# A two-layer hybrid decoder step: head loads in quarters, the table stage in fewer steps, chunks by way of DRAM and held norm products

## Chip, cores, metric

One core of one Trainium2 chip runs the whole step as one program. The metric is the device time of that program in microseconds (us), as the median of several runs; lower is better. Of the core's engines these matter here: TensorE (PE) for products and transposes, VectorE (DVE) and ScalarE (ACT) for elementwise work, GpSimd (POOL) for a few small operations, SyncE (SP), which issues most of the transfers.

## What is computed

The reference is one inference step of two layers on 256 prompt tokens and 8 x 8 sample tokens, in fp32. One layer, cut to what matters:

```
x  += 0.5 * SwiGLU_1(rms(x))
z   = rms(x) @ w_in            -> u (512) | q (512) | k (128) | v (128)
y_ssm  = GLU(gelu(Re(C h_t) + D u_t)),  h_t = Abar h_{t-1} + Bbar u_t   # 32 groups x 16 channels, 64 complex states each
y_attn = sliding-window attention over 128 keys, 8 heads, a sink per head
x  += concat(rms(y_ssm), rms(y_attn)) @ w_out
x  += 0.5 * SwiGLU_2(rms(x))
x  += (p @ w_ple_proj) * sigmoid(rms(x) @ w_ple_gate)
```

Then a final RMS norm. The width is 1024, the FFN's 2816. Besides the tokens' outputs the last keys and values and the last states are returned.

## The kernel before

All 320 tokens (256 + 64) lie along the free axis, channels on the 128 partitions, so x is 8 tiles of 128x320. To keep fp32 accuracy each weight block and each input is split into a high and a low part, and a 128x128 block of a product takes three PE instructions (mm3, lines 182 to 184: high x high, high x low, low x high), here called products. A weight tile of 128x1024 is loaded by SP into one of four raw buffers (wfetch, line 150), ACT makes the high part (line 163), DVE the low one (line 164), two tiles ahead of use.

A norm (class Norm, line 190) is not applied ahead of a product. ACT squares each tile (line 210), DVE adds the squares (line 216), and finish sums over partitions with three tiny PE products (line 244); DVE scales (line 247), POOL takes the power -1/2 (line 249), and three transposes spread the result over partitions (line 267). The spread is placed behind LATER = 22 further products, and the result multiplies the products' outputs when they are evacuated. For the two output norms in the mixer (attn_norm, ssm_norm, lines 929 and 934) the inputs themselves are scaled, so the following products depend on the spread.

Each layer runs FFN1, mixer, FFN2 and the per-layer embedding (ple). The FFN (line 272) has two halves of 11 blocks: gate and up products, then 8 down blocks. The S5 tables (powers of Abar, the block-Toeplitz table tt, the input table wb, the output table wc) are made by a generator, prep, in small steps, one after each FFN block (step, line 145): layer 0's beside FFN1, layer 1's beside FFN2 of layer 0. It writes tables to DRAM (wb_d, wc_d, kt_d, tt_d); tt_d is first filled with zeros, and then eight copies of ever shorter pieces go into it. At its end come doublings of cosine and sine tables (ect, est, lines 579 to 584) and a correction that renormalizes both (lines 590 to 595).

In the mixer (mix, line 601) tokens are grouped in chunks of 8: 40 chunks. u, evacuated as u2 (channel on partitions), must become U, where a partition is (position in the chunk, channel in the group). chunk_in does this on PE, per 8 groups: 8 transposes (line 669), two ACT copies, 8 transposes (line 674), an ACT copy; then the table products with wb (line 680). rotate (line 693) is a chain of ten DVE operations per 8 groups that turns these, scans over chunks and gives the states H. chunk_out multiplies U and H with tt and wc (line 872), transposes back (line 883) and applies D, gelu and a split. Attention runs in six units, four prompt and two sample: scores, softmax, flip (transposes of the probabilities), mix.

The string MIXSEQ sets the order in which all this is written: p0 to p9 are blocks of the input projection (q0: p0 and p1 together), i chunk_in, r rotate, s, f, m scores, flip and mix of a unit, y a step of chunk_out, z the ple projection, g the GLU, a and n the output norms, A and S the output projection, t and w table loads, v value transposes, x the load of p. Tile's scheduler then puts the instructions of each engine in one fixed order, which follows the written order closely but not exactly.

At the start x comes in three pieces (lines 1017 to 1026), the first weight in two halves, and POOL squares and adds the tiles of the first norm (line 1030).

## Time and profile before

| | us |
|---|---|
| median of 3 runs | 1287.34 (1287.19 to 1287.66) |
| the profiled execution | 1286.57 |
| its span in the profile | 1284.8 |
| PE busy | 1257.4 (98%) |
| DVE busy | 911.0 (71%) |
| ACT busy | 598.9 (47%) |
| POOL busy | 81.5 (6%) |

Busy time overlaps between engines. A PE instruction's shown duration (0.31 us for a product) is longer than the distance between two of them, since they are pipelined: what a product costs is read from the distance of starts, or from the number of products in a window without waits. The granted clock in a window is a share of 2.4 GHz; where it is 0.50 the clock was 1.2 GHz. The records of the clock begin at its first change, so the windows show 1.00 ahead of it whatever it was; there the distance of products tells.

### The profile page before, as it was taken

Reading aid. Unit: us, or ns where it says so; the run is one execution under the profiler, and the core shown is the slowest. Engines: PE = TensorE matmul, PEld = TensorE weight load, DVE = VectorE, ACT = ScalarE, POOL = GpSimd, SP = SyncE. Lnnn points to the kernel's source line nnn. Section 1 sums busy time; section 2 is a strip of 40 time slices with the busy share of each in tenths; the row PEclk is TensorE's granted clock in tenths of the full one; section 3 lists DMA queues with packets and bytes.
Section 4 is the critical chain, followed back from the end, with each engine's and each line's share of the span. In section 5 each row is a group of like instructions: output and inputs, shape, how many; then the busy total and the mean of one; then the engine's idle time right before and its main releaser. Section 6 shows DMA issues by size and latency. Waiting matters only on the chain.

```text
span 1284.8 us, 22994 instructions
## 1 busy us (share of the span) xinstructions
PE 1257.4 (98%) x9153; PEld 1231.1 (96%) x9153; DVE 911.0 (71%) x1609; ACT 598.9 (47%) x984; POOL 81.5 (6%) x96
## 2 busy tenths in 40 slices
PE   7999999899999999999999999999999999999996
PEld 7999999898899999999999999999888999999996
DVE  6588776978786878788785555557877755555575
ACT  5443433455764443344653333345476543333454
POOL 4300002001004000010000000000000000000000
PEclk9999999999999999999999999999999999999998
DMA  7836666354254468654444454345432444454351
GB/s 251 314 125 204 240 208 212 120 197 144 76 192 147 150 194 256 219 189 141 166 174 151 129 154 174 136 115 188 164 106 99 147 151 135 142 180 141 113 174 41
DMA packets 74620, 210.62 MB, mean 164 GB/s; under 512 B 8545, under 2 KB 18497, under 8 KB 74481
## 3 DMA queue, kind: packets, MB, share of 16 engines
q1 hardware_dynamic: 72560, 203.22, 47.8%
q0 software_dynamic: 1664, 5.28, 1.3%
q8 instruction: 72, 1.18, 0.4%
q10 hardware_dynamic: 288, 0.66, 0.1%
q14 instruction: 36, 0.29, 0.1%
HBM read 191.78 MB, written 19.69 MB: 165 GB/s over the span
## 4 chain that ended last, share of the span: by engine, by line
PE 89%; DVE 6%; issue 3%; ACT 1%; POOL 1%; DMA 0%; SPq 0%; POOLq 0%; DVEq 0%; ACTq 0%
PE pt L182 17%; PE pt L184 17%; PE pt L183 17%; PE pc L182 11%; PE pc L184 11%; PE pc L183 11%; DVE wl L164 2%; PE pa L872 1%; PE pa L500 1%; POOL r L249 1%; DVE s L704 0%; DVE s L703 0%; DMA xa<-xT 0%; PE pa L883 0%; PE pa L244 0%
## 5 line engine op out<-in xcount | busy, mean ns | idle before, releaser
L163 ACT ACTIVATE wh<-wr 128x1024 fp32r<-128x1024 f32 (+3 forms) x365 | 350.9, 963 | 556.3 <-issue 302.0
L184 PE MATMUL pt<-big,wl 128*128 128x320 f32 x1584 | 492.6, 311 | 4.3 <-DVE wl L164 4.3
L182 PE MATMUL pt<-big,wh 128*128 128x320 f32 x1584 | 493.4, 312 | 0.0
L183 PE MATMUL pt<-big,wh 128*128 128x320 f32 x1584 | 492.2, 311 | 0.0
L164 DVE TENSOR_TENSOR wl<-wr,wh 128x1024 fp32r<-128x1024 f32 (+3 forms) x365 | 403.1, 1107 | 100.5 <-ACT wh L163 98.5
L182 PE MATMUL pc<-big,wh 128*128 128x320 f32 x992 | 310.7, 314 | 6.7 <-ACT wh L163 6.0
L183 PE MATMUL pc<-big,wh 128*128 128x320 f32 x992 | 308.8, 312 | 0.0
L184 PE MATMUL pc<-big,wl 128*128 128x320 f32 x992 | 308.2, 311 | 0.0
L184 PEld LDWEIGHTS pt<-big,wl 128*128 128x128 f32 x1584 | 298.8, 189 | 6.0 <-DVE wl L164 5.5
L183 PEld LDWEIGHTS pt<-big,wh 128*128 128x128 f32 x1584 | 299.1, 189 | 0.5
L182 PEld LDWEIGHTS pt<-big,wh 128*128 128x128 f32 x1584 | 298.8, 189 | 0.7 <-issue 0.4
L182 PEld LDWEIGHTS pc<-big,wh 128*128 128x128 f32 x992 | 187.2, 189 | 9.6 <-ACT wh L163 6.2
L183 PEld LDWEIGHTS pc<-big,wh 128*128 128x128 f32 x992 | 187.1, 189 | 1.2 <-DVE big L226 1.2
L184 PEld LDWEIGHTS pc<-big,wl 128*128 128x128 f32 x992 | 187.2, 189 | 0.6 <-issue 0.3
L291 DVE TENSOR_TENSOR fa<-pt,ft 128x320 f32<-128x320 f32 x88 | 43.0, 489 | 91.0 <-PE pt L184 90.5
L288 DVE TENSOR_TENSOR ft<-pc,r 128x320 f32<-128x320 f32 x88 | 42.6, 488 | 53.6 <-PE pc L184 53.5
L334 DVE SCALAR_TENSOR_TENSOR fd<-pt,r 128x320 f32<-128x320 f32 x64 | 31.3, 490 | 31.6 <-PE pt L184 31.6
L249 POOL TENSOR_TENSOR r<-ms,mhalf 107x3 f32<-107x3 f32 x13 | 17.1, 1319 | 565.0 <-DVE ms L247 565.0
L225 ACT ACTIVATE big<-xa,prm 128x320 fp32r<-128x320 f32 x64 | 35.3, 559 | 31.4 <-DVE xa L335 17.4
L295 ACT ACTIVATE big<-fa 128x320 fp32r<-128x320 f32 x88 | 40.2, 459 | 14.6 <-DVE fa L291 14.5
L289 ACT ACTIVATE ft<-ft 128x320 f32<-128x320 f32 x88 | 40.0, 458 | 13.1 <-DVE ft L288 13.0
L226 DVE SCALAR_TENSOR_TENSOR big<-xa,prm,big 128x320 fp32r<-128x320 f32 x64 | 37.9, 599 | 8.4 <-ACT big L225 8.4
(246 smaller groups left out, 904.6 us busy)
## 6 DMA issues: line engine op xcount, KB each, us to landing
wr<-f1u SPq DMA_DIRECT2D x44, 512.0 KB, 3.2
wr<-f2g SPq DMA_DIRECT2D x44, 512.0 KB, 3.3
wr<-f2u SPq DMA_DIRECT2D x44, 512.0 KB, 3.3
wr<-f1g SPq DMA_DIRECT2D x43, 512.0 KB, 3.3
wr<-f1d SPq DMA_DIRECT2D x32, 384.0 KB, 3.1
wr<-f2d SPq DMA_DIRECT2D x32, 384.0 KB, 3.1
wr<-f1d SPq DMA_DIRECT2D x32, 320.0 KB, 2.9
wr<-win SPq DMA_DIRECT2D x20, 512.0 KB, 3.8
```

Source lines behind the costliest of these rows:

```text
L163: S.activation(h[:, c], raw[:, c], AF.Copy)
L164: i = V.tensor_tensor(lo[:, c], raw[:, c], h[:, c].bitcast(F32), op=OP.subtract)
L182: PE.matmul(ps, h[:, c], xh, start=start and k == 0, stop=False)
L183: PE.matmul(ps, h[:, c], xl, start=False, stop=False)
L184: PE.matmul(ps, lo[:, c], xh, start=False, stop=stop and k == n - 1)
L225: S.activation(h, src, AF.Copy, scale=g)
L226: V.scalar_tensor_tensor(lo, src, g, h.bitcast(F32), op0=OP.mult, op1=OP.subtract)
L288: V.tensor_tensor(t, pg, r, op=OP.mult)
L289: S.activation(t, t, AF.Silu)
L291: V.tensor_tensor(a, pu, t, op=OP.mult)
L295: S.activation(h, a, AF.Copy)
L334: V.scalar_tensor_tensor(t, pd, 0.5, r, op0=OP.mult, op1=OP.mult)
```

## The change

**Head.** The parameters, x in four quarters (three issued by ACT, one by SP) and quarters (128x256) of the first two weights are loaded first. 14 products on a zeroed tile (NWARM) stand ahead on PE. The first weights and x are split quarter by quarter, and the first FFN block (head=True) is computed in four groups of two input tiles, alternating between gate and up; the block m=2 uses another PSUM buffer. The squares of x move from POOL to ACT, their sums to DVE, behind the first block.

**Table stage.** kt_d gets 112 columns of zeros, and tt_d is written in eight full copies of 128 columns instead of being filled with zeros. The doublings of ect and est stand ahead of the b and c tables; the correction is applied once, to the first column, before the doublings. The reversed powers are copied by 16 small ACT instructions. The generator has 29 steps (36 before).

**Chunks.** chunk_in's transposes go. shuffle (u in MIXSEQ) writes the four u2 blocks to a DRAM tile ud and reads U back with eight transfers, one per position in the chunk; a row of such a read is 40 values. MIXSEQ starts with the input projection of u, then k, v and the queries, with the scores and rotates behind. p, z and g are held behind the last table product (behind).

**Norms.** LATER is 18. The output norms pass 12: the next 12 products are held behind the norm's sums, and the spread stands behind them.

The diff, cut to its core:

```diff
+    for q in range(4):
+        (S if q < 3 else nc.sync).dma_start(xa[:, 2 * q : 2 * q + 2], I["xT"][:, 2 * q : 2 * q + 2])
+        for raw, src in zip(first, firstw):
+            headdma.append(nc.sync.dma_start(raw[:, 256 * q : 256 * q + 256],
+                                             src[:, 256 * q : 256 * q + 256]).ins)
...
+    for _ in range(NWARM):
+        PE.matmul(pz[:, :T], zr_[:, :P], zr_, start=True, stop=True)
...
-LATER = 22
+NWARM = 14
+LATER = 18
...
     def mm3(ps, h, lo, off, pairs, start, stop):
...
+            with tc.issue_after(held[0]) if held else nullcontext():
+                PE.matmul(ps, h[:, c], xh, start=start and k == 0, stop=False)
...
-            waiting.append([LATER, later])
+            waiting.append([hold or LATER, later])
+            if hold:
+                held[:] = [mm.ins, hold]
...
-                    for k0, k1 in ((0, KCUT), (KCUT, 8)):
+                    ks = (0, 2, 4, 6, 8) if head else (0, KCUT, 8)
+                    for k0, k1 in zip(ks, ks[1:]):
...
-            zt = wpool.tile([P, 1024], F32, name=nm("wr"), tag="wr", bufs=4)
-            PO.memset(zt, 0.0)
-            for ll in range(L):
-                nc.sync.dma_start(tt_d[ll].rearrange("p (b c) -> p b c", b=4),
-                                  zt.unsqueeze(1).to_broadcast([P, 4, 1024]))
+            zt = auxt("sx", [P, 4, 112])
+            PO.memset(zt, 0.0)
+            for ll in range(L):
+                nc.sync.dma_start(kt_d[ll].rearrange("(p b) c -> p b c", b=4)[:, :, 0:112], zt)
...
+        V.tensor_tensor(t, uc, uc, op=OP.mult)
+        V.tensor_tensor(er, us, us, op=OP.mult)
+        V.tensor_tensor(t, t, er, op=OP.add)
+        V.tensor_scalar(t, t, -0.5, 1.5, op0=OP.mult, op1=OP.add)
+        V.tensor_tensor(ct_[:, :, 1], uc, t, op=OP.mult)
+        V.tensor_tensor(sn_[:, :, 1], us, t, op=OP.mult)
...
+        for k in range(8):
+            cp(prr[:, 7 - k], pr[:, k])
+            cp(pir[:, 7 - k], pi[:, k])
...
-            dst = tt_d[l][(7 - i) * 16 : (8 - i) * 16, :].rearrange("p (g c) -> p g c", c=P)
-            PO.dma_start(dst[:, :, i * 16 :], src[:, :, : (8 - i) * 16])
+            dst = tt_d[l][i * 16 : i * 16 + 16, :].rearrange("p (g c) -> p g c", c=P)
+            PO.dma_start(dst, src[:, :, (7 - i) * 16 : (7 - i) * 16 + P])
...
-        for c0 in (0, 16):
-            cc, ss = ct_[:, :, c0 : c0 + 16], sn_[:, :, c0 : c0 + 16]
-            q1, q2 = auxt("s", [P, G, 16]), auxt("p", [P, G, 16])
-            V.tensor_tensor(q1, cc, cc, op=OP.mult)
...
+        def shuffle(k):
+            for gb in range(4):
+                drain(gb)
+                nc.sync.dma_start(ud[gb * P : gb * P + P], u2[:, gb])
+            src = ud.rearrange("(g p) j c -> j p g c", p=16)
+            for j in range(8):
+                nc.sync.dma_start(U[j * 16 : j * 16 + 16], src[j])
...
-                    PE.transpose(px[:NC, s * P : (s + 1) * P], u2[:, gb, 7 - (hf * 4 + s), :], ident)
...
-                PE.transpose(pu[:, g * NC : (g + 1) * NC],
...
-            na.finish(lambda ra: [na.cut(m, ya[:, m, :], ra) for m in range(4)])
+            na.finish(lambda ra: [na.cut(m, ya[:, m, :], ra) for m in range(4)], 12)
...
-MIXSEQ = 'w0 q0 p3 i0 p2 i2 r0 w1 i3 r2 i1 p8 r3 r1 t1 p9 v t2 p5 t0 e x p4 y0 s0 s1 w2 f0 p6 m0 p7 s2 f1 t3 m1 s3 f2 m2 y0 w3 y0 y1 s4 f3 y1 m3 s5 z0 f4 z1 y1 z2 z3 y2 f5 y2 y3 m4 y3 y2 z4 y3 z5 z6 m5 a g0 g1 A0 n z7 A1 A2 S0 S1 S2 A3 S3'
+MIXSEQ = 'w0 q0 p2 p3 u p8 e p9 v p4 i0 s0 p5 i1 r0 t0 s1 f0 x p6 i2 r1 w1 m0 f1 s2 p7 i3 r2 t1 m1 y0 f2 s3 z0 r3 y0 t2 m2 f3 z1 y0 w2 y1 m3 s4 z2 y1 f4 s5 y1 t3 w3 z3 m4 f5 y2 y2 z4 y2 y3 m5 y3 y3 a z5 z6 g0 g1 A0 n z7 A1 A2 S0 S1 S2 A3 S3'
```

What this moves on the engines, at three places, as the order of each engine's instructions shows it. pc, pt, po and pa are PSUM tiles, big the activations, wh and wl the halves of a weight; line numbers of after are some 20 to 30 higher.

First, PE at the start of the program; big are halves of x. Before:

```order
L182 MATMUL pc_182<-big_110,wh_119 128x320
L183 MATMUL pc_182<-big_111,wh_119 128x320
L184 MATMUL pc_182<-big_110,wl_120 128x320
L182 MATMUL pc_182<-big_110,wh_119 128x320
L183 MATMUL pc_182<-big_111,wh_119 128x320
L184 MATMUL pc_182<-big_110,wl_120 128x320
```

After:

```order
L105 MATMUL po_102<-zr 128x320 x14
L202 MATMUL pc_194<-big_146,wh_142 128x320
L203 MATMUL pc_194<-big_147,wh_142 128x320
L202 MATMUL pt_195<-big_146,wh_144 128x320
L203 MATMUL pt_195<-big_147,wh_144 128x320
L204 MATMUL pc_194<-big_146,wl_143 128x320
L202 MATMUL pc_194<-big_146,wh_142 128x320
L204 MATMUL pt_195<-big_146,wl_145 128x320
L202 MATMUL pt_195<-big_146,wh_144 128x320
```

The zero products come ahead, and the products of gate (pc) and up (pt) alternate, both weights being needed at once.

Second, PE in the mixer of layer 0. Before, L669 and L674 are the chunk transposes and L680 the table products of the first chunk, and pt_3154 is the fourth block of the input projection:

```order
L669 MATMUL pa_3108<-ident,big_2975 40x128 x4
L669 MATMUL pa_3114<-ident,big_2975 40x128 x4
L182 MATMUL pt_3154<-big_2514,wh_3005 128x320
L183 MATMUL pt_3154<-big_2515,wh_3005 128x320
L184 MATMUL pt_3154<-big_2514,wl_3006 128x320
L182 MATMUL pt_3154<-big_2798,wh_3005 128x320
L183 MATMUL pt_3154<-big_2799,wh_3005 128x320
L184 MATMUL pt_3154<-big_2798,wl_3006 128x320
L182 MATMUL pt_3154<-big_2798,wh_3005 128x320
L674 MATMUL pa_3120<-ident,sx_3107 128x40 x8
L183 MATMUL pt_3154<-big_2799,wh_3005 128x320
L184 MATMUL pt_3154<-big_2798,wl_3006 128x320
```

After, pc_3274 is p4, L781 and L783 are unit 0's scores, L707 the first table products, and pc_3345 is p5:

```order
L204 MATMUL pc_3274<-big_2848,wl_3196 128x320
L781 MATMUL pt_3320<-kv_3224,big_3020 128x256
L783 MATMUL pt_3320<-kv_3224,big_3020 128x128
L781 MATMUL pt_3324<-kv_3224,big_3020 128x256
L783 MATMUL pt_3324<-kv_3224,big_3020 128x128
L707 MATMUL pa_3300<-big_3018,wb_3009 64x40 x16
L202 MATMUL pc_3345<-big_2643,wh_3230 128x320
```

No transposes are left, and the first table products stand behind the query block and the first scores.

DVE at the first rotate of layer 0's mixer; wl is a weight's low half. Before (L703 to L713 belong to rotate, L659 is k's evacuation):

```order
L703 TENSOR_TENSOR s_3221<-big_2977,est_2527 64x256
L704 TENSOR_TENSOR s_3221<-big_2977,est_2527 64x256
L164 TENSOR_TENSOR wl_3388<-wr_3385,wh_3387 128x1024
L707 TENSOR_TENSOR s_3221<-s_3221 128x256
L708 SCALAR_TENSOR_TENSOR s_3221<-dec_2523,s_3221 128x256
L702 TENSOR_TENSOR s_3221<-s_3221,ect_2526 128x256
L703 TENSOR_TENSOR s_3221<-s_3221,est_2527 64x256
L704 TENSOR_TENSOR s_3221<-s_3221,est_2527 64x256
L712 TENSOR_TENSOR big_2979<-s_3221 128x8x31
L713 TENSOR_TENSOR fin_2980<-s_3221 128x8
L702 TENSOR_TENSOR s_3275<-big_2977,ect_2526 128x256
L703 TENSOR_TENSOR s_3275<-big_2977,est_2527 64x256
```

After (unit 0's softmax has just ended, L730 to L740 are rotate 0, L1003 splits the ple input, L685 evacuates p5, for which unit 1's scores wait):

```order
L730 TENSOR_TENSOR s_3389<-big_3019,ect_808 128x256
L731 TENSOR_TENSOR s_3389<-big_3019,est_809 64x256
L732 TENSOR_TENSOR s_3389<-big_3019,est_809 64x256
L1003 TENSOR_TENSOR big_3436<-pj_3434,big_3436 128x320
L735 TENSOR_TENSOR s_3389<-s_3389 128x256
L1003 TENSOR_TENSOR big_3436<-pj_3434,big_3436 128x320
L736 SCALAR_TENSOR_TENSOR s_3389<-dec_805,s_3389 128x256
L730 TENSOR_TENSOR s_3389<-s_3389,ect_808 128x256
L731 TENSOR_TENSOR s_3389<-s_3389,est_809 64x256
L732 TENSOR_TENSOR s_3389<-s_3389,est_809 64x256
L740 TENSOR_TENSOR big_3021<-s_3389 128x8x31
L685 TENSOR_TENSOR big_3020<-pc_3345,r_3138 128x320
```

Rotate 0 has moved behind the softmax of the first unit, and the evacuation of p5 behind rotate 0.

Third, PE at the attention norm of layer 0. Before, pc_4109 is a GLU block, L244 are the sums and L267 the spread:

```order
L184 MATMUL pc_4064<-big_2993,wl_3829 128x320
L182 MATMUL pc_4109<-big_2993,wh_3965 128x320
L244 MATMUL pa_4032<-ones,acc_4021 107x1 x3
L183 MATMUL pc_4109<-big_2994,wh_3965 128x320
L184 MATMUL pc_4109<-big_2993,wl_3966 128x320
L182 MATMUL pc_4109<-big_2993,wh_3965 128x320
L267 MATMUL pa_4077<-ident,r_698_4038 128x107 x3
L183 MATMUL pc_4109<-big_2994,wh_3965 128x320
```

After, L877 and L882 are the end of the last unit's mix, L911 the last chunk's transposes, L269 the sums and pc_3986 the first of two ple blocks:

```order
L877 MATMUL po_3850<-p_3866,vtok_3032 64x128 x2
L882 MATMUL po_3850<-p_3866,vc_3029 64x32 x8
L911 MATMUL pa_3950<-ident,sx_3919 128x40 x8
L269 MATMUL pa_3978<-ones,acc_3967 107x1 x3
L202 MATMUL pc_3986<-big_3436,wh_3546 128x320
L203 MATMUL pc_3986<-big_3436,wh_3546 128x320
L204 MATMUL pc_3986<-big_3436,wl_3547 128x320
L202 MATMUL pc_3986<-big_3436,wh_3546 128x320
L203 MATMUL pc_3986<-big_3436,wh_3546 128x320
L204 MATMUL pc_3986<-big_3436,wl_3547 128x320
```

The sums stand directly behind the last unit, and all 12 products of the two ple blocks follow them before the spread (L294).

## Rows read from the trace of the kernel before

**Rows 1.** Windows: busy us (count) of PE, PEld, DVE, ACT, POOL, clock, DMA, GB/s.

```profile
0.00:32.00 32.00, 25.04 (x127) 22.71 (x128) 20.59 (x23) 17.48 (x27) 14.93 (x27) 1.00 0.70 250
32.00:64.00 32.00, 32.00 (x220) 32.00 (x219) 18.09 (x25) 13.73 (x20) 12.09 (x6) 1.00 0.85 314
...
224.00:256.00 32.00, 27.88 (x175) 26.91 (x174) 31.90 (x76) 12.90 (x23) 0.00 (x0) 0.95 0.40 124
```

**Rows 2.** Timeline of PE: start us, duration us, what, [idle before].

```profile
5.99 0.64 PE L182 MATMUL pc<-big,wh 128*128 128x320 f32 x1 [5.99 <-ACT wh L163]
...
18.28 0.47 PE L183 MATMUL pt<-big,wh 128*128 128x320 f32 x1
18.55 0.47 PE L184 MATMUL pt<-big,wl 128*128 128x320 f32 x1
...
19.57 0.31 PE L182 MATMUL pt<-big,wh 128*128 128x320 f32 x1
```

**Rows 3.** What PE waited for between 220 and 262: total us, times, longest.

```profile
PE pt L184 <- DVE wl L164: 4.1, 3, 1.9
```

**Rows 4.** Windows, two microseconds behind the second of these waits.

```profile
242.00:244.00 2.00, 2.00 (x9) 2.00 (x8) 2.00 (x4) 1.55 (x3) 0.00 (x0) 0.50 0.66 247
```

**Rows 5.** Windows, the mixer of layer 0 in two stretches.

```profile
267.48:323.07 55.59, 54.38 (x518) 48.38 (x517) 45.79 (x89) 31.08 (x68) 5.62 (x7) 1.00 0.46 158
323.07:391.08 68.01, 66.46 (x572) 62.93 (x573) 51.55 (x99) 46.49 (x100) 4.26 (x6) 1.00 0.37 127
```

**Rows 6.** Windows, the start.

```profile
6.00:12.00 6.00, 5.26 (x14) 3.72 (x15) 4.47 (x7) 3.77 (x7) 3.58 (x4) 1.00 1.01 398
```

**Rows 7.** Timeline around the attention norm: ACT's squares, the power, the spread.

```profile
344.95 0.82 ACT L210 ACTIVATE sq<-big 128x320 f32<-128x320 f32 x2
...
348.62 1.06 POOL L249 TENSOR_TENSOR r<-ms,mhalf 107x3 f32<-107x3 f32 x1 [13.11 <-DVE ms L247]
...
349.74 0.49 PE L267 MATMUL pa<-ident,r 107*128 107x107 f32 x3 [0.86 <-POOL r L249]
```

**Rows 8.** Timeline of DVE, one operation of the table correction.

```profile
241.24 0.68 DVE L590 TENSOR_TENSOR s<-ect 128x512 f32<-128x512 f32 x1
```

**Rows 9.** Timeline of PE, the first chunk and the products behind.

```profile
273.51 1.03 PE L669 MATMUL pa<-ident,big 128*40 128x128 f32 x8 [0.16 <-DVE big L652]
274.30 0.39 PE L182 MATMUL pt<-big,wh 128*128 128x320 f32 x1
...
275.49 0.69 PE L674 MATMUL pa<-ident,sx 40*128 40x40 f32 x8
276.11 0.42 PE L183 MATMUL pt<-big,wh 128*128 128x320 f32 x1
```

**Rows 10.** Timeline of SP, two weight loads issued in a row.

```profile
1.65 0.90 SPq L159 DMA_DIRECT2D wr<-f1g  x2
```

**Rows 11.** DMA issues: count, KB each, median us from issue to landing.

```profile
wbd<-p SPq DMA_DIRECT2D x16, 256.0 KB, 2.6
...
ktd<-kc SPq DMA_DIRECT2D x16, 32.0 KB, 1.7
```

**Rows 12.** Timeline of DVE: rotate 0 begins, rotate 1 from its first to last.

```profile
278.54 0.42 DVE L702 TENSOR_TENSOR s<-big,ect 128x256 f32<-128x256 f32 x1 [2.87 <-ACT big L82]
...
284.72 0.41 DVE L702 TENSOR_TENSOR s<-big,ect 128x256 f32<-128x256 f32 x1
...
289.28 0.17 DVE L713 TENSOR_TENSOR fin<-s 128x8 f32<-128x8 f32 x1
```

**Rows 13.** Groups of DVE's instructions, 267.48 to 323.07: busy us, mean ns, idle before.

```profile
L164 DVE TENSOR_TENSOR wl<-wr,wh 128x1024 fp32r<-128x1024 f32 x10 | 12.1, 1222 | 1.1 <-ACT wh L163 1.1
L756 DVE SCALAR_TENSOR_TENSOR s<-pt,maskp 128x384 f32<-128x384 f32 x8 | 4.2, 550 | 0.5 <-PE pt L755 0.4
...
L767 DVE TENSOR_TENSOR s<-s,dn 128x512 f32<-128x512 f32 (+1 forms) x6 | 3.1, 553 | 0.1
```

**Rows 14.** What PE waited for between 262 and 395.

```profile
PE pa L267 <- POOL r L249: 1.5, 2, 0.9
```

More of the change, by code (lines that the diff above doesn't have):

```diff
@@ L1 @@
 import math
-from contextlib import ExitStack
+from contextlib import ExitStack, nullcontext
 import numpy as np
@@ L174, in wtake @@
         return wready.pop(0)
-    waiting = []
+    waiting, held = [], []
     def mm3(ps, h, lo, off, pairs, start, stop):
@@ L950, in mix @@
         for o in seq:
-            ops[o[0]](int(o[1:] or 0))
+            with tc.issue_after(behind[0]) if behind and o[0] in "pzg" else nullcontext():
+                ops[o[0]](int(o[1:] or 0))
         shp = [P, G, 8]
```

207 lines of the change are left out of this document (100 added, 107 removed).

## The prediction

> **What bounds the kernel now.** I read the page first: TensorE (PE) is busy 98% of the span and the chain that ended last is 89% PE, so only what makes PE wait, or gives it less to do, can move the time. The windows then give the price of a product: 220 products of 128x320 in 32 us without one wait [rows 1], 145.5 ns each. Counting products per window against that price leaves three places where time is lost. At the **start** the first 32 us hold 127 products instead of 220 [rows 1]: 93 x 0.1455 = 13.5 us gone. Two reasons are in the timeline: the first product starts at 5.99, waiting for the first weight, and products then follow 0.27 us apart (18.28 to 18.55), the 1.2 GHz level, until 19.5, from where the pitch is that of 2.4 GHz [rows 2]. At the **end of the first FFN** of layer 0 PE waits three times for the low half of a weight, 4.1 us in all [rows 3], and behind the second wait the granted clock is 0.50 for a window of 2 us [rows 4]; counted in products, 45 are missing between 224 and 256 (175 against 220 [rows 1]), 45 x 0.1455 = 6.5 us. In the **mixer** (123.6 us from T0, the sums of its input norm at 267.48, to those of the next norm at 391.08; layer 1 the same) PE is busy 54.38 of 55.59 and 66.46 of 68.01 us [rows 5]: 2.76 us of waits, and the rest is work. VectorE (DVE) is busy 45.79 of the first 55.59 us, which will matter. Everything else, the long FFN stretches and the tail, the change leaves as it is.
>
> **Start.** The order shows 14 products on zeros ahead of the first real one; they need only a small memset and copy, so they run from about 1.5 us and, at 0.27 us, end near 5.3. The quarters (128 KB of each weight, 320 KB of x) let the first real product start right behind. What then bounds is the transfers: x, the parameters and the first two weights are 2.4 MB, and the queues moved 398 GB/s between 6 and 12 us [rows 6]: 6 us, behind some 3.5 until the first transfers run at that rate. Nothing in the change makes these bytes faster; they are in near 10, the splits of the last quarter take 1 us more, and the 12 products that need them end near 12.5. By then 48 products stand, worth 7.0 us: loss 5.5. The next two weights (1 MB) are in at about 12.5 and split at 13.5, nearly one more us of waiting. So 6.3 us are lost instead of 13.5. One thing is new: the order puts only 3 products between the first norm's sums and its spread, where 24 stood. POOL's power alone takes about 1 us, and at an output norm a spread with 3 products ahead of it waited 0.86 [rows 7]; I take 0.9 (0.8 to 1.8). Start: **-6.3**, between -3 (the clock rises late: 13 us of products at 0.27 are 6.5 us over their price, so half of it stays) and -8.5 (products follow the quarters without a gap).
>
> **Table stage.** The Newton correction was 12 DVE operations of 512 elements a layer, up to 0.68 us each [rows 8], and becomes six on one column; two 2 MB writes of zeros become two of 229 KB. In layer 0 DVE's order has no table operation left between the weight splits of the last eight down blocks, and there the three waits stand [rows 3]. With only splits, residual adds and norm work DVE has the mix it has from 32 to 64 (18.09 of 32 us [rows 1]). So the 6.5 us go: **-6.5**, between -5.5 (a step that moved forward delays one split) and -6.9. Layer 1's tables lie beside FFN2, where no PE wait stands; nothing there. The 16 added ACT copies a layer are small and ACT is busy 13.73 of 32 us [rows 1]: nothing, and 1 us at most if a split stands behind them.
>
> **Chunking by way of DRAM.** Per chunk PE drops 8 transposes that hold it from 273.51 to 274.30 and 8 from 275.49 to 276.11 [rows 9]: 0.79 + 0.62 = 1.4 us, four chunks 5.6 us a layer. ACT's 12 copies a layer go too; PE was hardly waiting for them. Instead SP issues 4 writes and 8 reads, some 0.45 us each [rows 10]. The last chunk is evacuated about 9 us after T0, a weight load ahead of its write waits for a buffer till about T0+10.8, the write takes up to 2.6 us and a read 1.7 to 2.6 by the nearest rows [rows 11]: U is there at T0+17.7 to 19.5. The order wants it first for the table products behind s0's scores, at T0+20.9 (120 products x 0.1455 = 17.5; sums, spread and value transposes 1.6; q's evacuation 0.7; scores 1.1). So the trip is hidden. On SP, the loads of the GLU and output weights stand behind the reads; they are used 40 us later. A row of these reads is 160 bytes. The Trainium skill, "DMA: Bandwidth & Descriptors", Specifications, says that transfers under 512 bytes do not reach line rate; no row here shows how slow 160 bytes are; by that rule the reads land later, which is rival E.
>
> **The mixer's order.** This is where I don't give the 5.6 us. The first y needs the rotates, 4.24 us each (284.72 to 289.45 with one evacuation of 0.49 in it [rows 12]), the softmaxes, six operations of 0.55 us a unit, 3.3, and weight splits of 1.22 [rows 13]. Before, rotate began 11 us after T0 (278.54 [rows 12]). Now rotate 0 stands behind s0's softmax, and s0 behind five weight blocks: it starts at about T0+24, and DVE idles some 7.5 us before. DVE's work up to y0 hardly changes. From T0+20.9: softmax 3.3 and 0.65 for ACT's exponentials, rotate 4.24 with two ple splits 1.0, and only then the evacuation of p5, which s1's scores wait for: PE is done with p5 and its table products at T0+26.6, the evacuation at T0+29.8, a **new wait of about 3.2 us**. After that a unit costs DVE 3.3 + 4.24 + 0.49 + 1.22 = 9.3 us and PE 24 products (3.5), table products 1.1, scores 1.1, flips 0.8, mix 0.7 = 7.2: DVE paces until the fourth rotate, with 0.6 to 1.9 us of waiting at each flip, partly covered by the products of z and y that stand between. First y evacuated at T0+54 to 57.5; before, T0+55.6. From there PE has 67.4 us (68.0 before). Net **-0.8 a layer**, -1.6 in all; without these waits it would be -5.6, and they may add up to 3 more than what goes.
>
> **Output norms.** Before, PE waited 1.5 us a layer for POOL's power at the two norms [rows 14], with 3 and 10 products between. Twelve are 1.75 us, so 0.1 to 0.5 of the wait remains. But the sums of the attention norm now stand right behind m5 and y3's transposes. The copy of m5's result and four squares on ACT, 0.41 each [rows 7], the last addition 0.49 and the gaps are about 3.2 us; y3 covers 0.7. So PE waits about 2.4 us at the sums, and the held products, which need nothing of it, may not go ahead. This is in the 67.4. Eighteen products at the other norms are 2.6 us, more than the 1.3 to 2.2 that I count for a power and its ways: 0 to +0.2.
>
> **Sum.** The profiled run took 1286.57 (span 1284.8, 1.8 around it), 0.8 below the median of 1287.34; the steps are differences and go to the median: -6.3 - 6.5 - 1.6 = -14.4, **1272.9 us**. Its own range (start -3 to -8.5, table -5.5 to -6.9, mixers -4 to +2) is 1266 to 1280.
>
> **Rivals.** B, the mixers gain what PE loses in work: DVE fits its work into the gaps, 2 x (5.6 + 1.2 of norm waits) = -13.6 instead of -1.6: 1261. For it: PE owns the chain; against it: DVE's 45.79 of 55.59. Chance 0.13. C, the zero products don't bring the clock up: it rose 13.5 us after the first product in the trace, though it came back 3.4 us after its fall at 241.4 (that fall is the 0.50 of [rows 4]); the slow pitch then stays to 15 us and more and the start gives -3: 1276. Chance 0.12. D, the new waits grow and the clock falls behind them as in [rows 4]: the mixers lose 3 to 4 each: 1281. Chance 0.13. E, the other side: the 160-byte reads are slow. U is needed at T0+20.9 and DVE's order gives it 1.6 us more; from T0+22.5 every us delays the first rotate and with it y, 1 us a layer. Slower than before from U at about T0+30 on, reads of some 13 us instead of 2; at 16, 1290. Transfers of like size in the trace take 1.7 to 2.6 us [rows 11], so 0.05. Last, that the parts do nothing where they stand (quarters that wait for each other, splits as late as before): 1285, 0.02.
>
> **Numbers.** Forecast 0.55, B 0.13, C 0.12, D 0.13, E 0.05, no effect 0.02. The range takes in C, most of D and the near half of B: 1261 to 1282. A measurement of this kernel tells 0.2% (2.6 us) from none. Faster: all but E and "no effect", 0.93; same 0.03; slower 0.04.
>
> **What would show it.** In the profile after: products at 0.145 us from about 10 us and a first spread that waits under 2 us (start); no wait for a low half between 220 and 262 (table); from the mixer norm's sums to FFN2's sums 122 to 125 us, with a wait at s1's scores and one of over 2 us at the attention sums (mixer). Table products that wait for DMA would mean E; a mixer under 119 us would prove my DVE argument wrong, and products at 0.27 beyond 15 us my start.

## The result, and the profile after

| | before | after |
|---|---|---|
| median, us | 1287.34 | 1294.03 (5 runs, 1291.4 to 1295.51) |
| ratio to before | | 1.0051, 95% interval 1.0039 to 1.0063 |
| profiled execution, us | 1286.57 | 1291.40 |
| its span, us | 1284.8 | 1289.6 |
| from the start to the mix norm's sums of layer 0, us | 267.48 | 261.29 |
| mixer of layer 0, sums of its norm to those of FFN2's | 123.60 | 129.07 |
| mixer of layer 1 | 123.56 | 128.54 |

The change made the kernel 0.5% slower, where 1.1% faster was forecast. Start and table stage gave 6.2 us, the two mixers took 10.5. FFN2 of layer 0, where the tables of layer 1 are made, took 0.8 more (240.5 for 239.7).

**The mixer.** The windows of after, cut at the last product of the last attention unit (m5), in layer 0 and layer 1 (columns as in [rows 1]):

```profile
261.29:336.00 74.71, 68.97 (x691) 62.24 (x690) 58.91 (x119) 40.70 (x97) 8.69 (x10) 0.95 0.50 153
336.00:390.36 54.36, 50.20 (x341) 49.35 (x338) 38.36 (x69) 31.50 (x59) 2.84 (x2) 0.94 0.38 128
893.11:967.12 74.01, 68.56 (x691) 61.62 (x690) 58.74 (x119) 40.92 (x97) 4.06 (x7) 0.95 0.54 153
967.12:1021.65 54.53, 50.37 (x340) 49.52 (x337) 38.36 (x69) 31.50 (x59) 2.83 (x2) 0.94 0.31 107
```

The same cut in before:

```profile
267.48:343.68 76.20, 74.99 (x774) 66.35 (x774) 60.96 (x123) 48.25 (x114) 7.05 (x11) 1.00 0.40 138
343.68:391.08 47.40, 45.85 (x321) 44.96 (x318) 36.38 (x67) 29.31 (x54) 2.83 (x2) 1.00 0.42 146
```

Up to m5 after is 1.5 to 2.2 us shorter, but 12 products of ple (1.76 us) now come behind that cut, so it lost 0.3 in layer 0 and gained 0.4 in layer 1. Behind m5 it needs 7.0 us more, 5.2 without these 12 products. The granted clock, 1.00 in every mixer window of before, is 0.94 and 0.95 here. What PE waited for in layer 0's mixer (total us, times, longest; L707 are the first table products, which wait for U: the row names the load of a GLU weight, but the wait goes in e6, where only the reads of U change):

```profile
PE pa L269 <- DVE acc L241: 2.7, 1, 2.7
PE pt L781 <- DVE fin L741: 2.4, 1, 2.4
PE pa L911 <- ACT sx L82: 2.4, 4, 1.1
PE pa L707 <- DMA wr<-glu: 1.1, 1, 1.1
PE pt L781 <- DVE big L685: 0.6, 1, 0.6
PE pa L294 <- POOL r L274: 0.2, 1, 0.2
```

The spread waits of before (1.5 us, [rows 14]) are down to 0.2, as the held products meant. In their place stand the sums of the attention norm (L269, 2.7), unit 1's scores (L781, 2.4, behind a rotate) and the last step of chunk_out (L911). The timeline of all engines at the attention sums:

```profile
335.57 0.66 PE L882 MATMUL po<-p,vc 128*64 128x32 f32 x16
...
337.33 0.69 PE L911 MATMUL pa<-ident,sx 40*128 40x40 f32 x8 [1.10 <-ACT sx L82]
...
337.54 0.82 ACT L235 ACTIVATE sq<-big 128x320 f32<-128x320 f32 x2
...
339.25 0.45 ACT L235 ACTIVATE sq<-big 128x320 f32<-128x320 f32 x1
...
340.08 0.48 DVE L241 TENSOR_TENSOR acc<-acc,sq 128x320 f32<-128x320 f32 x1
...
340.71 1.21 PE L269 MATMUL pa<-ones,acc 128*107 128x1 f32 x6 [2.69 <-DVE acc L241]
...
341.78 0.61 PE L202 MATMUL pc<-big,wh 128*128 128x320 f32 x1
...
342.19 0.47 PE L203 MATMUL pc<-big,wh 128*128 128x320 f32 x1
...
345.13 0.49 PE L294 MATMUL pa<-ident,r 107*128 107x107 f32 x3
```

m5 ends at 336.2, and until 341.8 PE does two short things: 8 transposes and the sums, each after a wait. Then the 12 held products stretch from 341.78 to 345.1: 0.27 us apart, the 1.2 GHz level, where at the 2.4 GHz pitch they would take 1.75 us. The window of that stretch says the same (clock 0.50):

```profile
338.40:345.22 6.82, 4.51 (x19) 4.50 (x20) 3.11 (x8) 2.21 (x5) 1.07 (x1) 0.50 0.00 0
```

In the mixers of before the clock never fell. In after it fell three times in layer 0 (at 283.8, 294.0 and 338.4) and twice in layer 1 (915.2, 969.9). What the fall behind m5 cost is read from the 88 products between the attention norm's sums and those of the next norm: both layers of after, and layer 1 of e5 (below), where the same work stands in one stretch at full clock:

```profile
340.71:357.00 16.29, 16.17 (x98) 15.78 (x98) 10.66 (x21) 8.79 (x18) 1.07 (x1) 0.86 0.13 39
971.83:988.30 16.47, 16.35 (x98) 15.96 (x98) 10.66 (x21) 8.79 (x18) 1.05 (x1) 0.85 0.13 39
```

```profile
975.72:989.90 14.18, 14.06 (x99) 13.70 (x98) 10.18 (x20) 8.33 (x17) 1.05 (x1) 1.00 0.15 46
```

That is 2.1 us in layer 0 and 2.3 in layer 1; for some 2 us of the 6.83 at half clock PE stood still anyway.

**Start and tables.** Windows of after:

```profile
0.00:32.00 32.00, 28.48 (x165) 27.25 (x166) 17.06 (x33) 15.37 (x31) 8.64 (x19) 1.00 0.64 223
32.00:64.00 32.00, 30.61 (x207) 30.09 (x206) 26.64 (x82) 18.98 (x40) 6.67 (x5) 1.00 0.65 216
...
224.00:256.00 32.00, 32.00 (x220) 32.00 (x219) 25.85 (x44) 19.09 (x32) 0.00 (x0) 1.00 0.59 186
```

224 to 256 holds 220 products, 175 before [rows 1]: the table tail's loss is gone whole. But 32 to 64 holds 207, 220 before. Followed by the number of the product, after is ahead of before by 5.95 us at product 96 (22.40 against 28.35), by 3.5 at product 110, by 1.6 at 150, 0.8 at 500, behind by 0.65 at 1000, and ahead by 6.2 at the last one ahead of the mixer. So the head gained 5.95, the first norm's bubble took back 2.45 (1.5 of it waits; the sums themselves, which before has ahead of product 96, are in it too), new waits in the table stage 4.1, and the table tail gave 6.85. The timeline of PE, with the waits between 20 and 110 us:

```profile
23.60 0.70 PE L269 MATMUL pa<-ones,acc 128*107 128x1 f32 x6 [0.75 <-DVE acc L241]
25.57 0.49 PE L294 MATMUL pa<-ident,r 107*128 107x107 f32 x3 [0.73 <-POOL r L274]
33.22 0.41 PE L202 MATMUL pc<-big,wh 128*128 128x320 f32 x1 [0.69 <-ACT wh L171]
34.48 0.42 PE L204 MATMUL pc<-big,wl 128*128 128x320 f32 x1 [0.71 <-DVE wl L172]
...
84.50 0.41 PE L204 MATMUL pc<-big,wl 128*128 128x320 f32 x1 [0.47 <-DVE wl L172]
104.19 0.42 PE L202 MATMUL pt<-big,wh 128*128 128x320 f32 x1 [0.79 <-ACT big L322]
```

The last two stand where DVE has its table operations one behind the other now (15.8 and 15.9 of 16 us busy from 64 to 80 and from 80 to 96, 11.9 of 12 from 96 to 108). What is behind the pair at 33 shows on POOL and ACT:

```profile
25.48 5.44 POOL L421 TENSOR_TENSOR dt<-econ,lam 128x32 f32<-128x32 f32 x1
...
31.87 0.23 ACT L82 ACTIVATE prr<-pwr 128x32 f32<-128x32 f32 x1 [9.10 <-POOL pwr L402]
...
32.12 1.04 ACT L171 ACTIVATE wh<-wr 128x1024 fp32r<-128x1024 f32 x1
```

One of the small copies that the change adds stood at the head of ACT's queue for 9.1 us, since its source is set by POOL behind a power of 5.44 us, and the next weight split stood behind the copy. The same copy, made for layer 1's tables, stands in FFN2 of layer 0:

```profile
399.01 0.23 ACT L82 ACTIVATE prr<-pwr 128x32 f32<-128x32 f32 x1 [7.03 <-POOL pwr L402]
```

### The profile page after: what moved, and what is told of

It is laid out like the page before. It is cut to its first block, busy times and chain, and to the rows that moved or that the text cites. A ratio compares the mean times of both kernels' runs of the same rounds, so it can differ in the third digit from the quotient of the medians.

```text
span 1289.6 us, 22827 instructions
## 1 busy us (share of the span) xinstructions
PE 1252.8 (97%) x9039; PEld 1230.9 (95%) x9039; DVE 896.5 (70%) x1607; ACT 592.4 (46%) x1001; POOL 67.8 (5%) x85
## 4 chain that ended last, share of the span: by engine, by line
PE 79%; DVE 11%; issue 3%; ACT 2%; DMA 2%; POOL 2%; SPq 0%; POOLq 0%; DVEq 0%; ACTq 0%
PE pt L203 16%; PE pt L202 16%; PE pt L204 16%; PE pc L202 9%; PE pc L204 9%; PE pc L203 9%; DVE wl L172 2%; ACT wh L171 1%; POOL dt L421 1%; DMA wr<-glu 1%; PE pa L269 1%; POOL r L274 1%; PE pa L569 1%; DVE big L323 1%; ACT sx L82 0%
## 5 line engine op out<-in xcount | busy, mean ns | idle before, releaser
L323 DVE TENSOR_TENSOR big<-fa,big 128x320 fp32r<-128x320 f32 x88 | 42.6, 485 | 1.1 <-ACT big L322 1.1
```

The costliest lines, as they stand in the source:

```text
L323: V.tensor_tensor(lo, a, h.bitcast(F32), op=OP.subtract)
```

## The experiments

The column us has medians; before ran beside each group of experiments at 1287.0 to 1287.2. The other columns are read from the one profiled execution of each kernel, which can lie up to 3 us from the median (after 2.6 below it, e1 1.8 above, e14 3.0 below), so differences of 1 to 2 us between them are not firm.

| run | us | mixer of layer 0, 1 | up to m5 | behind m5 |
|---|---|---|---|---|
| before | 1287.3 | 123.6, 123.6 | 76.2, 76.2 | 47.4, 47.4 |
| after | 1294.0 | 129.1, 128.5 | 74.7, 74.0 | 54.4, 54.5 |
| e1_nohold | 1286.6 | 126.4, 127.5 | 74.4, 75.8 | 52.0, 51.7 |
| e2_oldmix | 1291.6 | 127.2, 128.4 | 76.5, 76.5 | 50.7, 51.9 |
| e3_transposes_neworder | 1297.0 | 131.9, 135.0 | 76.0, 77.5 | 55.8, 57.5 |
| e4_memset_first | 1291.2 | 130.6, 130.5 | 75.3, 76.0 | 55.3, 54.5 |
| e5_fill | 1291.7 | 130.6, 128.2 | 74.1, 74.7 | 56.5, 53.5 |
| e6_contiguous | 1294.2 | 130.5, 129.2 | 74.8, 74.0 | 55.7, 55.2 |
| e7_head_table | 1279.7 | 124.1, 124.0 | 76.5, 76.5 | 47.6, 47.6 |
| e9_order | 1284.3 | 127.0, 124.8 | 79.0, 76.8 | 48.0, 48.0 |
| e12_less_dve | 1290.8 | 128.8, 128.7 | 73.1, 73.3 | 55.7, 55.3 |
| e13_later | 1276.1 | 122.5, 122.4 | 76.6, 76.5 | 46.0, 45.9 |
| e14_hold | 1288.7 | 128.6, 127.2 | 76.6, 76.5 | 52.0, 50.7 |
| e15_hold_fill | 1283.3 | 125.7, 125.7 | 76.6, 76.5 | 49.2, 49.2 |

With the old order 294 products stand behind m5, with the new one 306 (298 in e1, 291 in e9).

### Whose loss: the stages ahead, the order, the held products

**e7_head_table**: head, tables and LATER 18 of the change (with the two memsets of e4, further down) and the old mixer: chunks by transposes, the order string of before, nothing held.

```diff
-MIXSEQ = 'w0 q0 p2 p3 u p8 e p9 v p4 i0 s0 p5 i1 r0 t0 s1 f0 x p6 i2 r1 w1 m0 f1 s2 p7 i3 r2 t1 m1 y0 f2 s3 z0 r3 y0 t2 m2 f3 z1 y0 w2 y1 m3 s4 z2 y1 f4 s5 y1 t3 w3 z3 m4 f5 y2 y2 z4 y2 y3 m5 y3 y3 a z5 z6 g0 g1 A0 n z7 A1 A2 S0 S1 S2 A3 S3'
+MIXSEQ = 'w0 q0 p3 i0 p2 i2 r0 w1 i3 r2 i1 p8 r3 r1 t1 p9 v t2 p5 t0 e x p4 y0 s0 s1 w2 f0 p6 m0 p7 s2 f1 t3 m1 s3 f2 m2 y0 w3 y0 y1 s4 f3 y1 m3 s5 z0 f4 z1 y1 z2 z3 y2 f5 y2 y3 m4 y3 y2 z4 y3 z5 z6 m5 a g0 g1 A0 n z7 A1 A2 S0 S1 S2 A3 S3'
...
+                    PE.transpose(px[:NC, s * P : (s + 1) * P], u2[:, gb, hf * 4 + s, :], ident)
...
-            na.finish(lambda ra: [na.cut(m, ya[:, m, :], ra) for m in range(4)], 12)
+            na.finish(lambda ra: [na.cut(m, ya[:, m, :], ra) for m in range(4)])
```

> Only head, table stage (with the memsets of the first powers ahead of POOL's long power) and LATER 18 of the change; the mixers with PE transposes, the order string of before and no held products. Theory (the mixers alone turn the gain into a loss): the mixers take 123 to 124 us again, the mix norm's sums come 7.5 to 8 us earlier than before: 1279 to 1281 us. Rival (part of the mixer's loss is due to head and tables): over 1283 us.

Measured 1279.7 (ratio 0.9945, 0.9930 to 0.9960): the mixers are those of before to 0.5 us, and the mix norm's sums come 7.8 us earlier. The mixers alone turned the gain into a loss. The stretch behind m5, layer 0:

```profile
336.19:383.78 47.59, 45.86 (x321) 44.97 (x317) 36.40 (x67) 29.19 (x54) 2.87 (x2) 1.00 0.45 145
```

**e2_oldmix**: the same, but with the held products kept (and the memsets of e4 further down not yet made; its chunk positions are reversed against the tables, which moves values, not time). Its edit against e7:

> The changed kernel with the mixer's chunking by PE transposes and its order string as before; head, table stage, LATER 18 and the held products as in the change. Theory (chunking and order cost the mixers what they lost): each mixer falls from 129 to 123 to 124.5 us (the held products may add up to 1 at the attention sums), the whole 1282 to 1285 us, no fall of the clock between 290 and 300. Rival (the mixers are slower because of what the earlier stages left behind, or because of the held products alone): mixers stay at 127 to 129, 1289 to 1294 us.

```diff
-            na.finish(lambda ra: [na.cut(m, ya[:, m, :], ra) for m in range(4)])
+            na.finish(lambda ra: [na.cut(m, ya[:, m, :], ra) for m in range(4)], 12)
...
-                    PE.transpose(px[:NC, s * P : (s + 1) * P], u2[:, gb, hf * 4 + s, :], ident)
+                    PE.transpose(px[:NC, s * P : (s + 1) * P], u2[:, gb, 7 - (hf * 4 + s), :], ident)
```

Measured 1291.6, mixers 127.2 and 128.4: neither as the theory said. The old order with the held products loses 3.6 and 4.8 us a mixer, all but 0.3 of it behind m5. My theory had blamed the chunking and its order alone; the rival's "held products alone" was nearer.

**e1_nohold**: the change without holding.

```diff
-            na.finish(lambda ra: [na.cut(m, ya[:, m, :], ra) for m in range(4)], 12)
+            na.finish(lambda ra: [na.cut(m, ya[:, m, :], ra) for m in range(4)])
...
-            ns.finish(lambda rs: [ns.cut(m, yg[:, m, :], rs) for m in range(4)], 12)
+            ns.finish(lambda rs: [ns.cut(m, yg[:, m, :], rs) for m in range(4)])
```

> The changed kernel without the holding of 12 products at the two output norms; the spread stands 18 products behind the sums as at the other norms and nothing is held. Theory (the mixers lost 5.5 and 5.0 us because of new waits and of the 1.2 GHz stretches that follow each of them): the wait of 2.7 us at the attention sums goes and with it the 6.8 us at half clock behind it (worth some 2 us), in both layers, less about 1 us a layer of spread waits that come back: 1294.0 - 7 = 1287 us, no fall of the clock near 338 and 970. Rival (the wait only moves from the sums to the spread, the hold costs nothing): 1293 to 1295.

Measured 1286.6 (0.9996, 0.9987 to 1.0006), 7.4 less than after by the medians, as the theory gave it in sum; the two mixers of the profiled executions differ by 2.7 and 1.0 only. And the clock fell at 338.8 and 970.3 all the same, so half of the reason given was wrong: PE waits there also without the hold (0.9 us for ACT's evacuation of a ple block, 0.3 ahead of it). What is left of the new mixer, then, still costs 2.2 and 3.5 us a layer against e7: its order, the DRAM trip and the holding of p, z and g behind the last table product, which no run takes away by itself.

**e3_transposes_neworder**: the change with its order, but chunk_in as in e7 (positions reversed as in e2).

```diff
-                nc.sync.dma_start(ud[gb * P : gb * P + P], u2[:, gb])
...
-                nc.sync.dma_start(U[j * 16 : j * 16 + 16], src[j])
...
+                    PE.transpose(px[:NC, s * P : (s + 1) * P], u2[:, gb, 7 - (hf * 4 + s), :], ident)
...
+                PE.transpose(pu[:, g * NC : (g + 1) * NC],
+                             X[:, g].rearrange("c i p -> c (i p)"), ident[:NC, :NC])
```

> The changed kernel with its new order, but the chunks made by PE transposes instead of by way of DRAM. Theory (the order, not the trip through DRAM, makes most of the waits): the wait for U goes (1.1 and 2.7 us), the waits at s1's scores and at the sums stay, the transposes (5.6 us a layer) fill part of the waits: 1296 to 1302 us. Rival (the DRAM trip is the cause: its transfers and the wait for U): 1284 to 1288 us, mixers back near 124.

Measured 1297.0 with mixers of 131.9 and 135.0: the new order with the transposes is the slowest of all, so the DRAM trip is not the cause; with it and without the transposes the mixers are 2.8 and 6.4 us shorter in this order. That difference is not the transposes' alone: this edit also takes away the holding of p, z and g behind the last table product, and in layer 1 of its profiled execution the clock was at half for 17.1 us.

### What the clock costs

**e5_fill**: the change with products on zeros in two of its waits.

```diff
+            if o == "s1":
+                with tc.issue_after(behind[0]):
+                    zeros(15)
...
+            with tc.issue_after(lastt[0]):
+                zeros(16)
             na.finish(lambda ra: [na.cut(m, ya[:, m, :], ra) for m in range(4)], 12)
```

> The changed kernel with 31 more products on zeros a layer, put where PE waits: 15 ahead of unit 1's scores, 16 ahead of the attention norm's sums (their result is not used). They are worth 4.5 us of PE at 2.4 GHz and fit into the two waits (2.4 and 2.7 us), so the path to DVE and ACT stays as it is. Theory (behind each wait PE pays again at the 1.2 GHz level: 3.4 us and 6.8 us stretches): the clock no longer falls at 294 and 338, the mixers lose 2 to 4 us, 1286 to 1290 us, though PE does more work. Rival (the clock does not care, the waits are the whole loss): 1294 to 1296 us, and falls of the clock where they were.

Measured 1291.7, between the two. In layer 0 the clock no longer fell at 283 to 297, but fell at 337.1, ahead of the filled place, and stayed at half for 10.2 us; in layer 1 it fell twice for 3.4 us. The 16 products ahead of layer 0's sums thus ran at half clock, 4.6 us instead of 2.3, and pushed the sums from 4.7 to 6.8 us behind m5. Not decided: the fall does not hang on one wait.

**e14_hold** and **e15_hold_fill**: e7 with the held products (the 12 of the change passed to both output norms), without and with 20 products on zeros in the one wait that they make. The edit of e15 against e14:

```diff
             for m in range(4):
                 na.stat(ya[:, m, :])
+            with tc.issue_after(lastt[0]):
+                zeros(20)
             na.finish(lambda ra: [na.cut(m, ya[:, m, :], ra) for m in range(4)], 12)
```

> Head and table stage alone with the old mixer, and only the 12 held products at the output norms added. Theory: the sums of the attention norm then stand right behind the last unit's mix and wait for ACT and DVE (3.3 us), the clock falls there in both layers (3.4 to 6.8 us), and from that mix to the sums of FFN2's norm a layer takes 50.5 to 52 us instead of 47.6: 1286 to 1288.5 us against 1279.7 without holding. Rival (the held products cost nothing when the rest is as before): 1279 to 1281 us.

> As e14_hold, with 20 products on zeros a layer (2.9 us at 2.4 GHz, their result not used) in the wait of 3.3 us ahead of the attention sums; the sums come no earlier by that. Theory (the clock's share is 1.2 to 1.5 us for each 3.4 us at half clock): no fall of the clock there, the stretch behind the mix falls to 49 to 49.5 us, 2 to 5 us less than e14_hold in all, though PE does 5.8 us more work. Rival (the clock falls all the same, or costs nothing): the same time or 0 to 3 us more than e14_hold.

Measured 1288.7 (1.0010, 1.0000 to 1.0019) and 1283.3 (0.9973, 0.9961 to 0.9984), so the theory of both, to 0.5 us. Layer 0 behind m5, e14: the wait, the half clock behind it, the rest:

```profile
334.92:337.83 2.91, 0.23 (x8) 0.11 (x4) 1.91 (x5) 2.48 (x7) 0.00 (x0) 1.00 0.00 0
337.83:344.66 6.83, 6.24 (x26) 6.20 (x27) 1.68 (x5) 0.54 (x2) 0.89 (x1) 0.50 0.00 0
344.66:386.93 42.27, 42.00 (x289) 41.50 (x288) 33.00 (x58) 26.32 (x46) 1.77 (x1) 1.00 0.49 164
```

and e15, with the zeros in the first line:

```profile
335.87:339.38 3.51, 3.35 (x29) 3.05 (x25) 2.40 (x6) 2.47 (x7) 0.00 (x0) 1.00 0.00 0
339.38:344.66 5.28, 5.28 (x39) 5.27 (x40) 2.54 (x7) 1.90 (x5) 0.89 (x1) 1.00 0.00 0
344.66:385.02 40.36, 40.10 (x275) 39.60 (x274) 31.54 (x55) 24.86 (x43) 1.77 (x1) 1.00 0.51 171
```

The sums start 3.5 us behind the last mix in both (338.42 and 339.38; the filled wait shows no gain of its own), yet the stretch behind m5 is 49.15 in both layers with the clock kept, and 52.0 and 50.7 without: 2.85 us for a stretch of 6.83 us at half clock (PE busy for 6.24 of it) and 1.6 for one of 3.41. PE does 40 useless products more and the kernel is 5.4 us faster. The wait itself costs 49.15 - 47.6 = 1.6 net of the spread waits it saves.

### What paces the mixer up to m5

**e6_contiguous**: U read in rows of 5 KB (the same bytes, in other places of U).

```diff
-            src = ud.rearrange("(g p) j c -> j p g c", p=16)
+            src = ud.rearrange("(k g) j c -> k (g j) c", g=4)
             for j in range(8):
-                nc.sync.dma_start(U[j * 16 : j * 16 + 16], src[j])
+                nc.sync.dma_start(U[j * 16 : j * 16 + 16], src[j * 16 : j * 16 + 16])
```

> The changed kernel with U read back from DRAM in rows of 5 KB (the same bytes in the same eight transfers, but not rearranged, so that U holds the values in another place). Theory (rows of 160 bytes make the reads land after 4.2 to 6.2 us): the reads land within 2 to 3 us and the waits for U (1.1 us in layer 0, 2.7 in layer 1) go: 2 to 4 us less, 1290 to 1292 us. Rival (the reads are late because they share the queues with the weight loads): landing stays over 4 us and the waits stay, 1294 us.

The reads landed in 2.7 us instead of 5.1, by the DMA issues of after and of e6:

```profile
big<-ud SPq DMA_DIRECT2D x16, 80.0 KB, 5.1
```

```profile
big<-ud SPq DMA_DIRECT2D x16, 80.0 KB, 2.7
```

PE's wait for U went, and the time stayed at 1294.2: the wait at unit 1's scores grew from 2.4 to 4.3 us instead. So the theory was right on the landing and wrong on the time: U was not on the path; DVE's chain up to p5's evacuation was. The two layers of after say the same: layer 1 got U 1.6 us later than layer 0, waited 2.7 us for it instead of 1.1 and not at all at unit 1's scores, and these started 31.6 us behind the sums there and 31.5 in layer 0.

**e12_less_dve**: three of the ten operations of each rotate, its second turn, left out.

```diff
-            turn(g)
```

> The changed kernel without the second turn of each rotate (three DVE operations of 0.42 us, twelve and 5.1 us a layer; the states it hands on are not the right ones). Theory (up to the last unit's mix DVE sets the pace, with the transposes gone): the stretch from the mix norm's sums to the last unit's mix, 74.7 and 74.0 us, shortens by 3 to 5 us, the stretch behind it stays at 54 to 55; 1284 to 1289 us. Rival (PE and its clock set the pace there): that stretch stays within 1 us, 1292 to 1294 us.

1290.8, between theory and rival: the stretch shortened by 1.6 and 0.7 us for 5.1 us of DVE work. Unit 1's scores came 1.4 us earlier (30.1 us after the sums instead of 31.5), as three operations give; those of units 2 and 3 came 1.2 us earlier in layer 0 and 0.3 in layer 1, though two and three rotates stand ahead of them. DVE alone is not the pace; from unit 2 on the chain goes through scores (PE), softmax (DVE and ACT), flips (PE) and copies (ACT), and I have not separated their shares.

**e9_order**: the change without its hold, with the memsets of e4 and another order: U by way of DRAM, k and two query blocks directly behind it (the scores take k from where the projection leaves it, since the value block now comes later).

```diff
+MIXSEQ = 'w0 q0 p2 p3 u p4 p8 e s0 p5 s1 p9 v i0 t0 f0 r0 p6 x m0 i1 w1 f1 r1 p7 m1 s2 i2 t1 y0 i3 y0 f2 r2 t2 m2 s3 y0 w2 y1 y1 z0 z1 f3 r3 m3 y1 t3 w3 s4 z2 y2 y2 f4 s5 z3 y2 m4 y3 y3 f5 z4 y3 m5 a z5 z6 g0 g1 A0 n z7 A1 A2 S0 S1 S2 A3 S3'
```

> Head and table stage of the change (memsets first, nothing held) with U by way of DRAM, but another order in the mixer: k and two query blocks directly behind u, the scores and softmaxes of units 0 and 1 while U travels, value block and table products behind them, and rotates in turn with flips, so that no evacuation of a query block stands behind a rotate before the scores that need it. Theory (the order of DVE's work made the waits, and the clock followed them): the mixers come under the 124.1 us of the old order, 118 to 121 us each, 1269 to 1275 us. Rival (without the transposes PE has too little dense work in this stretch, DVE paces it in any order and the clock falls): mixers of 124 to 128 us, 1279 to 1288 us.

1284.3, mixers 127.0 and 124.8: the rival. The waits at unit 1's scores and at the sums are gone, no wait is longer than 1.2 us, but there are eleven of 0.3 to 1.2 us, and the clock fell at 287.4 and 311.3. Behind m5 it is at 48.0, near the old order. In neither of the two orders did the 5.6 us of transposes come out of the mixer.

### Head and tables

**e4_memset_first**: the memsets of the first powers ahead of POOL's power.

```diff
         pr, pi = st("pwr", (P, 9, G)), st("pwi", (P, 9, G))
+        PO.memset(pr[:, 0, :], 1.0)
+        PO.memset(pi[:, 0, :], 0.0)
         dt = st("dt")
```

> The changed kernel with the two memsets of the first powers of the table stage ahead of POOL's long power operation (5.4 us) instead of behind it. Theory (ACT stood from 22.8 to 31.9 us at the first copy of the reversed powers, whose source POOL had not yet set, and the weight splits behind it came late): the two waits at 33 and 34 us go, 1.9 us less: 1292 us. Rival (SP is the cause: its zero writes of the table tile wait for POOL too, and the next weight loads stand behind them until 32.7): the waits stay or move by a few us, 1294 us, and two PE waits of about 1 us between 33 and 40.

The two waits at 33 and 34 us went, the mix norm's sums came 1.7 us earlier (259.59 against 261.29), and FFN2 of layer 0 took 239.7 again: ACT's queue was the cause of both losses, 2.5 us together. The time was 1291.2, 2.8 less than after; but in its profiled execution the mixers took 1.5 to 1.9 us more than in that of after, so the two stages carry this finding and not the median.

**e8_nowarm**: e7 with NWARM = 0.

```diff
-NWARM = 14
+NWARM = 0
```

> The kernel with head and tables alone, without the 14 products on zeros ahead. Theory (they bring the clock up earlier): first real product at 5.8 us as with them, clock up some 5 to 9 us later, 0.12 us for each product until then: 2 to 5 us slower than with them, 1282 to 1285 us. Rival (the clock follows the real products): within 0.5 us of the run with them.

1282.1, 2.4 more than with the zero products (four runs each, 1279.9 to 1282.7 against 1278.9 to 1280.3). In its profiled execution the clock rose at 11.1 us (6.1 with them), and the first norm's waits then brought it down for 6.8 us instead of 3.4; but the profiled executions of other kernels with the zero products show the rise anywhere from 4.8 to 11.3, so the medians carry this finding, as far as four runs can, and the single rise does not.

**e10_fafter**: e7 with the first norm's sums one tile later (FAFTER 6).

```diff
-FAFTER = (5, 3, 4)
+FAFTER = (6, 3, 4)
```

> The kernel with head and tables alone, with the first norm's sums one weight tile later (FAFTER 6 instead of 5), so that DVE's additions are done when PE comes to the sums and 10 products instead of 3 stand ahead of the spread. Theory (the bubble at the first norm, 1.25 + 0.9 us, and the 3.4 us at half clock behind it gave back part of the head's gain): no fall of the clock near 26 us, 2 to 3.5 us less than with head and tables alone, 1276 to 1278 us. Rival (the gate and up results then wait for the norm in PSUM and PE waits for a buffer instead): 1279 to 1281 us.

1279.3 against 1279.7, so no gain. The spread's wait went, but the sums then waited 1.8 us for DVE's last addition, as long as sums and spread together in e7 (1.1 + 0.7), and the clock fell at 25.9 as in e7 (26.6). What is late there are the additions; the place of the sums doesn't help.

**e13_later**: e7 with a later spread at the output norms (36 and 24 products behind the call) and nothing held.

```diff
-            na.finish(lambda ra: [na.cut(m, ya[:, m, :], ra) for m in range(4)])
+            na.finish(lambda ra: [na.cut(m, ya[:, m, :], ra) for m in range(4)], 36)
...
-            if hold:
-                held[:] = [mm.ins, hold]
```

> Head and table stage alone, old mixer, with the spread of the output norms written later (36 and 24 products behind the call of the norm, 18 at the others) and no products held: 11 products stand between sums and spread in the order instead of 3 and 9. Theory (what the change meant by its held products is to be had by a later spread, without tying the sums to a place): the spread waits, 1.7 us a layer, fall below 0.5; 1276 to 1278 us against 1279.7 with head and tables alone. Rival (the scaled inputs then come late for the output projection and PE waits there): 1279 to 1282 us.

1276.1 (0.9920, 0.9906 to 0.9935), mixers 122.5 and 122.4: the spread waits are gone from the list, 0.5 us came at one scaled input, and the sums stay where the scheduler finds them ready. This beats before by 0.8%, and the change by 1.4%.

## Why the prediction was wrong

The forecast was 21 us too low. By the profiled executions the two mixers make up 12.0 of it, the table stage 3.8, the start 2.8 and FFN2 of layer 0 0.8; the rest is the distance of these executions from their medians.

- **Start, -6.3 forecast, -3.5 measured.** The head itself gave 5.95 where the forecast had 7.2 (13.5 less 6.3): first real product at 5.80, pitch of 0.145 from 10.8 us. The slow pitch ended well ahead of 15 us and the zero products were worth 2.4 us, so rival C's condition did not hold, though the start came out near its -3. The larger miss is the bubble at the first norm, 0.9 forecast, 2.45 measured: I had priced the spread only, and the sums, too, had to wait for DVE's additions, which now come late.
- **Table stage, -6.5 forecast, -2.7 measured.** The tail gave 6.85. "Nothing, and 1 us at most" for the ACT copies failed: 1.9 us here, and 0.8 in FFN2 of layer 0, where I had said "nothing there". I had looked at their length, not at what they wait for, and the weight split behind them in ACT's order waited with them (e4). "No table operation left there" was right, but the work had moved ahead, and at 84 and 104 us it took 2.2 back.
- **Chunking.** The first table products started at T0+21.7 and T0+23.3, where U was forecast for T0+17.7 to 19.5: the reads took 5.1 us and not 2, the writes 3.4 and not 2.6 at most, and PE waited 1.1 and 2.7. The Trainium skill, "DMA: Bandwidth & Descriptors", Specifications, says that transfers under 512 bytes do not reach line rate. The trace agrees in direction: 5.1 us in rows of 160 bytes, 2.7 in rows of 5 KB. Rival E was nevertheless not the cause, as e6 shows.
- **The mixer up to the first y** came as forecast in kind: s1's wait 2.4 in layer 0 (forecast 3.2; the terms given add up to T0+30.1 and so to 3.5), no gain from the transposes. But the first y came at T0+57.9 (319.14) and 57.2, the late end of the 54 to 57.5 forecast and 2.3 and 1.6 us later than before, where the net of -0.8 a layer needs it at 55.4. The reason given, DVE alone, is only part of it (e12); what the falls of the clock in this stretch add is not shown.
- **Behind the first y is the step that failed.** I gave PE 67.4 us from there; it took 71.2 and 71.4. Two terms were wrong. The waits: I had 2.4 us at the attention sums and 0.1 to 0.5 at the spreads; PE stood 5.0 us in all, 2.7 at the sums, 1.1 at y3's transposes and 1.2 in smaller waits. And the clock was put at nothing: only rival D named it, held unlikely at 0.13, at 3 to 4 us a layer in all. The fall behind m5 cost 2.1 and 2.3 us. Together that is 4 to 5 us a layer, against a miss of 3.8 and 4.0. Counted against before, m5 to FFN2's sums is 7.0 us longer: 1.76 for the 12 products, 2.5 for the waits (1.1 + 2.7 + 0.2 less the 1.55 of before), 2.1 for the clock and 0.7 for y3's 8 transposes, which before has ahead of m5.
- **Held products.** I saw that they may not go ahead, and priced that with the wait alone, 2.4 us less some 1.2 of spread waits. The hold takes from the scheduler the choice to place the sums where they are ready; in the old order that alone costs 4.4 and 3.2 us a layer behind m5 (e14 against e7), of which e15 shows 2.85 and 1.6 to be the clock.
- **The sums on record** have two slips. The terms of the range add up to 1268 to 1281, not 1266 to 1280; and rival E's reads of 16 us come to 1293 by its own rule of 1 us a layer, not 1290. Neither bears on what failed.

How much of the mixers' loss is the hold's depends on the order around it. By the medians it costs 9.0 us in the old order (e14 against e7) and 7.4 in the new one (after against e1). By the profiled executions, behind m5, it is 4.4 and 3.2 us a layer in the old order, and 1.2 and 1.6 in the new one when the 8 products that stand there more are taken off, since there the clock falls without the hold too. What is left of the new mixer without it loses 2.2 and 3.5 us a layer (e1 against e7).

What stays open: which engine paces units 2 and 3, what the holding of p, z and g does, and why the clock falls in stretches without any wait over 1.2 us (e1 at 338.8, e9 at 311.3). These have in common that PE runs small transposes and 40-column products with short gaps; no run here separates that from the gaps.

## What to carry to other kernels

A forced place for a reduction whose operands come late was paid twice here, in the wait and in the slow clock behind it; give the consumer more distance (e13) rather than hold what could run. A small instruction on an engine with a fixed order is priced by what it waits for and by what stands behind it. And work taken off the busiest engine is a gain only if the chain through the others is shorter too: here 5.6 us of PE work a layer went, and neither of two orders turned them into time.
